# Splitting 42 matmuls of the last block into halves of 256 columns, which moves TensorE's instruction fetches by 84 instructions

## The chip, the cores and the metric

The kernel runs on one core of a Trainium2 chip. The metric is the device time of one execution in microseconds (us); a quoted time is a median of several executions. The profiled execution also has a span, from the first to the last instruction of the program; here the time is some 2 us longer than the span. All executions told of here are marked fast (single ones: unknown), and the granted clock of TensorE (PE in the profile), as the mean of an execution, is 0.998 to 1.0 everywhere; the lower values in some windows below stand behind its last matmul.

Executions of one kernel differ by several tenths of a microsecond, mostly because the first 40 us, where inputs are loaded, never run quite alike. So besides the times this document uses a distance that leaves the beginning out: **from the start of the last matmul to the end of the last store packet**, both taken from the single records of the trace. It is called the *tail* below.

## The reference

```python
x: (16, 512, 768)   w1: (768, 3072)   b1: (3072,)   w2: (3072, 768)
y = np.matmul(x, w1) + b1
y = 0.5 * y * (1.0 + erf(y / np.sqrt(2.0)))
return np.matmul(y, w2).astype(np.float32)
```

## The kernel before

The 8192 rows are worked through in eight blocks of 1024. Both products use a seven-product scheme (Strassen's, in Winograd's form) in place of eight block products. A block of the first product has twelve units (`Unit1`), each with seven products of three matmuls of 512 columns:

```python
class Unit1:
    F = RH          # 512
    C = KQ          # 3
    ...
    def mm(self, p, dst, first, c0, c1):
        A11, A12, A21, A22 = blocks(self.sb)
        a, slot = {1: (A11, B11), ...}[p]
        for c in range(c0, c1):
            nc.tensor.matmul(out=dst[:, 0:RH], lhsT=w1_op(self.wt, slot)[:, c, :],
                             rhs=a[:, c, :], start=first and c == 0,
                             stop=c == self.C - 1, skip_group_check=True)
```

The second product of the last six blocks has seven units (`Unit3`), each with seven products of twelve matmuls of 192 columns. The rest of the output is stored at the end: four stores of 384 KB while the very last unit runs, then that unit's `store_quarter`, its `store(0)` in `p3`, and two small ones in `last`, one on SyncE and one on ScalarE:

```python
def p3(u):
    u.mm(3, bZ, False, 0, u.C)
    ...
        nc.vector.tensor_tensor(out=u.c12(), in0=u.bank(bZ), in1=u.bank(w), op=ADD)
        if u.ends:
            u.store(0)                       # 384 KB, the fifth full store
...
def last(self, banks):
    for t in range(2):
        self.mm(4, banks[t], True, 0, self.C, (t,))
        o = self.dst[:, 1, t, 0, :]
        tt(o, banks[t][:, t * N4:(t + 1) * N4], o, ADD)
        (nc.sync, nc.scalar)[t].dma_start(out=orr[...], in_=o)      # 96 KB each
```

## Time and profile before

| | before |
|---|---|
| time, median of 3 runs | 852.42 us (852.32 to 852.53) |
| span of the profiled run | 850.5 us |
| TensorE busy | 842.8 us, 99% |
| TensorE's instruction fetches | 51 packets of 16 KiB |
| last matmul starts | 845.02 us |
| last fetch starts | 844.30 us |
| last store packet ends | 848.97 us |

The page, the groups, SyncE's last stores and the windows of the end are shown line by line in the prediction below. A window is a stretch of time, and its DMA share is the mean over the core's sixteen DMA engines, so that a share of 0.06 is one engine at work and fifteen idle. Two more lines of the time line of before are needed later, TensorE's last group and ScalarE's store (start, length, engine, line, operation, count):

```profile
844.12 1.15 PE L518 MATMUL bX<-arena 128*128 128x192 f16 x12
```

```profile
845.70 0.38 ACTq L529 DMA_DIRECT2D out_dram<-arena  x1
```

### The profile page before, as it was taken

Reading aid. Unit: us, or ns where it says so; the run is one execution under the profiler, and the core shown is the slowest. Engines: PE = TensorE matmul, PEld = TensorE weight load, DVE = VectorE, ACT = ScalarE, POOL = GpSimd, SP = SyncE. Lnnn points to the kernel's source line nnn. Section 1 sums busy time; section 2 is a strip of 40 time slices with the busy share of each in tenths; the row PEclk is TensorE's granted clock in tenths of the full one; section 3 lists DMA queues with packets and bytes.
Section 4 is the critical chain, followed back from the end, with each engine's and each line's share of the span. In section 5 each row is a group of like instructions: output and inputs, shape, how many; then the busy total and the mean of one; then the engine's idle time right before and its main releaser. Section 6 shows DMA issues by size and latency. Waiting matters only on the chain.

```text
span 850.5 us, 16682 instructions
## 1 busy us (share of the span) xinstructions
PE 842.8 (99%) x6504; PEld 573.4 (67%) x6504; DVE 673.3 (79%) x1134; ACT 426.3 (50%) x700; POOL 94.8 (11%) x151
## 2 busy tenths in 40 slices
PE   8999999999999999999999999999999999999997
PEld 5444445796544897449964599545995469944797
DVE  5766679777857997679967799668996699957997
ACT  4777763231287413773247721577126861277511
POOL 5021100042200002000020000210002100010000
PEclk9999999999999999999999999999999999999999
DMA  9998796699998699977999599995999949984497
GB/s 224 203 282 173 163 222 230 235 203 219 368 340 185 216 338 364 290 163 266 335 366 292 125 298 342 360 288 108 316 350 347 259 143 323 359 308 146 122 316 255
DMA packets 144819, 222.11 MB, mean 261 GB/s; under 512 B 61964, under 2 KB 85444, under 8 KB 144740
## 3 DMA queue, kind: packets, MB, share of 16 engines
q1 hardware_dynamic: 117392, 178.85, 66.6%
q0 software_dynamic: 27168, 42.08, 22.3%
q8 instruction: 51, 0.84, 0.4%
q14 instruction: 28, 0.23, 0.1%
q10 hardware_dynamic: 180, 0.11, 0.0%
HBM read 181.78 MB, written 49.45 MB: 272 GB/s over the span
## 4 chain that ended last, share of the span: by engine, by line
PE 98%; DMA 1%; ACT 0%; DVE 0%; SPq 0%; issue 0%
PE bY L414 21%; PE bY L518 15%; PE bX L414 14%; PE bX L518 10%; PE bW L414 7%; PE bZ L414 7%; PE bZ L518 5%; PE bW L518 5%; PE bY L457 4%; PE bZ L457 2%; PE bW L457 2%; PE bY L606 2%; PE bX L606 1%; PE bX L457 1%; DMA arena<-in_x_dram 1%; PE bZ L606 1%
## 5 line engine op out<-in xcount | busy, mean ns | idle before, releaser
L210 DVE TENSOR_TENSOR arena<-arena 128x1536 f16<-128x1536 f16 (+6 forms) x638 | 410.1, 674 | 5.7 <-ACT arena L335 0.9
L414 PEld LDWEIGHTS <-arena 128*128 128x128 f16 x1974 | 192.5, 98 | 224.0 <-issue 0.2
L518 PEld LDWEIGHTS <-arena 128*128 128x128 f16 x3528 | 292.1, 98 | 8.2
L414 PE MATMUL bY<-arena 128*128 128x512 f16 x846 | 214.4, 379 | 0.0
L637 DVE TENSOR_TENSOR arena<-bY,arena 128x512 f32<-128x512 f32 (+1 forms) x102 | 69.4, 681 | 118.1 <-PE bY L414 88.0
L630 ACT COPY bY<-bX 128x512 f32<-128x512 f32 (+1 forms) x145 | 79.6, 549 | 118.1 <-DVE arena L567 87.9
L518 PE MATMUL bY<-arena 128*128 128x192 f16 x1500 | 138.3, 246 | 0.0
L414 PE MATMUL bX<-arena 128*128 128x512 f16 x564 | 138.2, 379 | 0.0
L430 ACT ACTIVATE arena<-arena,b1t 128x1024 f16<-128x1024 f32 x94 | 108.0, 1149 | 51.6 <-DVE arena L665 51.6
L650 ACT COPY arena<-bW 128x512 f32<-128x512 f32 (+1 forms) x149 | 81.9, 550 | 92.9 <-PE bW L518 43.9
L518 PE MATMUL bX<-arena 128*128 128x192 f16 x1020 | 93.1, 246 | 0.0
L665 DVE TENSOR_TENSOR arena<-bZ,arena 128x512 f32<-128x512 f32 (+1 forms) x102 | 69.3, 679 | 21.4 <-PE bZ L414 18.2
L550 POOL DMA_DIRECT2D out_dram<-arena x42 | 30.5, 728 | 409.7 <-DVE arena L661 374.1
L414 PE MATMUL bW<-arena 128*128 128x512 f16 x282 | 76.2, 379 | 0.0
L414 PE MATMUL bZ<-arena 128*128 128x512 f16 x282 | 76.2, 379 | 0.0
L681 ACT COPY bZ<-bY 128x512 f32<-128x512 f32 (+1 forms) x60 | 31.8, 529 | 80.8 <-PE bY L457 30.0
L435 ACT ACTIVATE arena<-bX,b1t 128x512 f16<-128x512 f32 x94 | 64.0, 680 | 9.8 <-PE bX L414 9.7
L435 ACT ACTIVATE arena<-bY,b1t 128x512 f16<-128x512 f32 x94 | 63.3, 674 | 0.0
L457 PEld LDWEIGHTS <-arena 128*128 128x128 f16 x432 | 42.2, 98 | 28.0 <-issue 0.2
L319 POOL DMA_DIRECT2D arena<-in_x_dram x60 | 33.5, 626 | 156.3 <-DMA arena<-arena 146.9
L518 PE MATMUL bZ<-arena 128*128 128x192 f16 x504 | 48.5, 246 | 0.0
L518 PE MATMUL bW<-arena 128*128 128x192 f16 x504 | 48.5, 246 | 0.0
(63 smaller groups left out, 426.4 us busy)
## 6 DMA issues: line engine op xcount, KB each, us to landing
arena<-w2s SPq DMA_DIRECT2D x299, 288.0 KB, 4.6
arena<-w1s SPq DMA_DIRECT2D x72, 672.0 KB, 6.8
out_dram<-arena POOLq DMA_DIRECT2D x46, 384.0 KB, 7.1
w2s<-arena SPq DMA_DIRECT2D x49, 288.0 KB, 4.4
arena<-in_x_dram POOLq DMA_DIRECT2D x60, 192.0 KB, 7.7
w1s<-arena SPq DMA_DIRECT2D x12, 672.0 KB, 6.6
arena<-in_w_dram POOLq DMA_DIRECT2D x17, 384.0 KB, 8.4
out_dram<-arena SPq DMA_DIRECT2D x13, 384.0 KB, 2.5
```

Source lines behind the costliest of these rows:

```text
L210: nc.vector.tensor_tensor(out=o, in0=a, in1=b, op=op)
L319: nc.gpsimd.dma_start(out=xhs[t], in_=xr[:, sb * 8 + t, :])
L414: nc.tensor.matmul(out=dst[:, 0:RH], lhsT=w1_op(self.wt, slot)[:, c, :], rhs=a[:, c, :], start=first and c == 0, stop=c == self.C - 1, ski ...
L430: nc.scalar.activation(out=self.G[1][:, hi, :, :], in_=self.tmp, func=GELU, bias=b1t[:, 2 * hi + 1:2 * hi + 2])
L435: nc.scalar.activation(out=self.G[0][:, hi, row, :], in_=bank[:, 0:RH], func=GELU, bias=b1t[:, 2 * hi:2 * hi + 1])
L457: nc.tensor.matmul(out=dst[:, 0:N2], lhsT=a, rhs=w[:, :, c, :], start=first and c == 0, stop=c == self.C - 1, skip_group_check=True)
L518: nc.tensor.matmul(out=dst[:, t * N4:(t + 1) * N4], lhsT=a, rhs=w[:, c, :], start=first and c == 0 and t == ts[0], stop=c == NQ - 1, skip_ ...
L606: nc.tensor.matmul(out=dst[:, t * N4:(t + 1) * N4], lhsT=a, rhs=self.w[q][:, c, :], start=first and c == 0 and t == 0, stop=c == NQ - 1, s ...
L630: nc.scalar.copy(out=bY[u.g % 2][:, 0:u.F], in_=bX[u.g % 2][:, 0:u.F])
L637: nc.vector.tensor_tensor(out=u.c22(), in0=bY[u.g % 2][:, 0:u.F], in1=w[:, 0:u.F], op=ADD)
L650: nc.scalar.copy(out=w[:, 0:u.F], in_=bW[:, 0:u.F])
L665: nc.vector.tensor_tensor(out=u.c12(), in0=bZ[:, 0:u.F], in1=w[:, 0:u.F], op=ADD)
```

## The change

Units 1 and 2 of the last block's first product issue each matmul as two of 256 columns. The result is the same; 42 matmuls and their 42 weight loads are added, 84 instructions, so that every block of 256 instructions that TensorE fetches afterwards begins 84 instructions earlier in the work. The intent is to move the fetches, not to change the arithmetic.

```diff
                 a, slot = {1: (A11, B11), ...}[p]
+                w = RH // (2 if self.sb + 1 == nsb and self.k in (1, 2) else 1)
                 for c in range(c0, c1):
-                    nc.tensor.matmul(out=dst[:, 0:RH], lhsT=w1_op(self.wt, slot)[:, c, :],
-                                     rhs=a[:, c, :], start=first and c == 0,
-                                     stop=c == self.C - 1, skip_group_check=True)
+                    for r in range(0, RH, w):
+                        nc.tensor.matmul(out=dst[:, r:r + w], lhsT=w1_op(self.wt, slot)[:, c, :],
+                                         rhs=a[:, c, r:r + w], start=first and c == 0 and r == 0,
+                                         stop=c == self.C - 1, skip_group_check=True)
```

## The prediction

> **What bounds the kernel now.** I read the page first: busy time, queues and the chain of work that ended last.
>
> ```profile
> PE 842.8 (99%) x6504; PEld 573.4 (67%) x6504; DVE 673.3 (79%) x1134; ACT 426.3 (50%) x700; POOL 94.8 (11%) x151
> ...
> q8 instruction: 51, 0.84, 0.4%
> ...
> PE 98%; DMA 1%; ACT 0%; DVE 0%; SPq 0%; issue 0%
> ```
>
> TensorE is the bound: 842.8 of 850.5 us, 98% of the chain. The queue marked "instruction" moved 51 packets, 0.84 MB, so 16 KiB each; 6504 matmuls and 6504 weight loads in 51 pieces make 255 instructions a piece, so this queue is TensorE's own. That is the thing the change wants to shift. Does a fetch ever hold TensorE? The rows of groups say no: the columns after the bar are busy us, mean ns, then idle us before.
>
> ```profile
> L414 PE MATMUL bY<-arena 128*128 128x512 f16 x846 | 214.4, 379 | 0.0
> L518 PE MATMUL bY<-arena 128*128 128x192 f16 x1500 | 138.3, 246 | 0.0
> ```
>
> No idle time stands before either kind. I also took the distance from each matmul's start to the next one's: all the excess over the usual distance sums to 1.9 us in the whole run, 1.2 of it in the first 100 us; in the last block one step of 0.08 us stands out, at 815.25 us, and its like is found once in each of the five blocks before, exactly 103 us apart, while the fetches fall at another phase in every block. So no fetch costs TensorE anything, and what is left to gain lies outside its busy time: the first 2 us, and the 5.2 us between its last matmul (845.3) and the end (850.5).
>
> So I read the end closely: SyncE's time line of the last stores, then windows (columns: window, its length, busy us of PE, PEld, DVE, ACT, POOL, granted clock, DMA share, GB/s).
>
> ```profile
> 839.65 3.26 SPq L550 DMA_DIRECT2D out_dram<-arena  x4
> 843.91 0.37 SPq L556 DMA_DIRECT2D out_dram<-arena  x1
> 844.90 1.04 SPq L550 DMA_DIRECT2D out_dram<-arena  x1
> 846.04 0.42 SPq L529 DMA_DIRECT2D out_dram<-arena  x1
> ```
>
> ```profile
> 838.00:840.50 2.50, 2.50 (x34) 2.50 (x32) 2.50 (x5) 0.48 (x1) 0.00 (x0) 1.00 0.03 10
> 840.50:841.60 1.10, 1.10 (x16) 1.10 (x15) 1.00 (x3) 0.00 (x0) 0.00 (x0) 1.00 0.93 344
> 841.60:842.00 0.40, 0.40 (x8) 0.40 (x6) 0.40 (x2) 0.00 (x0) 0.00 (x0) 1.00 0.35 123
> 842.00:845.80 3.80, 3.27 (x40) 3.04 (x37) 3.18 (x8) 0.00 (x0) 0.00 (x0) 1.00 1.00 349
> 845.80:846.40 0.60, 0.00 (x0) 0.00 (x0) 0.00 (x0) 0.00 (x0) 0.00 (x0) 1.00 0.06 15
> 846.40:848.30 1.90, 0.00 (x0) 0.00 (x0) 0.00 (x0) 0.00 (x0) 0.00 (x0) 0.85 0.92 316
> 848.30:849.00 0.70, 0.00 (x0) 0.00 (x0) 0.00 (x0) 0.00 (x0) 0.00 (x0) 0.50 0.06 21
> ```
>
> The reader is to see the two windows with a DMA share of 0.06, one engine of sixteen: 845.8 to 846.4 and 848.3 to 849.0. One DMA engine is behind the other fifteen, and the program waits for it twice. The single packet records say why: at 844.297 us the last instruction fetch, 16,384 B, starts on one engine and takes 1.241 us; on that engine no data packet starts until 845.524, and the next four of 1,536 B start 0.16 us apart, where the usual distance is 0.062 us. And the store issued at 844.90 took 1.04 us to issue where the others took about 0.4; it ended (845.95) only after the slow engine had moved three more packets. The same shows earlier: of the ten other DMA issues on SyncE after 211 us that took over 0.75 us, nine began 0.2 to 1.2 us after a fetch had begun, and the tenth 0.04 us before one. The last packets of fifteen engines end by about 848.28, the last of the slow one at 848.97.
>
> **What the Trainium skill says.** "Runtime: NRT & Kernel Launch", section Instruction fetch mechanics: the queue is refilled in 16 KiB blocks of 256 instructions, by a DMA queue that the sequencer drives, at a cost that is mostly hidden. The trace agrees with the block and with hidden, for TensorE; not for the stores behind it. "DMA: Bandwidth & Descriptors", section Queues, rings and completion order: every DMA engine takes its queue rows in turn, packet by packet. The trace agrees: the 16 KiB packet is one turn of 1.24 us. "TensorE: Matmul & The Clock Gate", section Back-to-back issue gap: N/2.4 + 2.5 ns between isolated warm matmuls, which is 215.8 ns at 512 columns and 109.2 at 256. "Advanced Engine Details and Errata", section Engine Queue Depths: 64 for TensorE; no view shows the depth directly.
>
> **The change, part by part.** *Added work.* Units 1 and 2 of the last block have 7 products of 3 matmuls each: 42 matmuls of 512 columns become 84 of 256, with 42 more weight loads. The order of the built program agrees: 13,093 TensorE rows for 13,009, and nothing moved on another engine. Both sizes stand in the trace of before (columns: start, length, what):
>
> ```profile
> 18.54 0.82 PE L786 MATMUL bY<-arena 128*128 128x256 f16 x6
> 19.19 0.82 PE L786 MATMUL bW<-arena 128*128 128x256 f16 x6
> ...
> 22.46 0.81 PE L414 MATMUL bW<-arena 128*128 128x512 f16 x3
> 23.11 0.81 PE L414 MATMUL bY<-arena 128*128 128x512 f16 x3
> ```
>
> Start to start that is 0.65 us for 6 matmuls of 256 and for 3 of 512; the records give 109 and 216 ns as medians, in agreement with the skill. So each split costs 2 x 109 - 216 = 2 ns, 42 of them 0.084 us, all on TensorE's path. The weight load (98 ns) hides under 109 ns, as it does under the 82.6 ns of the 192-column matmuls. **Cost: +0.09 us.**
>
> *Moved fetches.* Every fetch boundary after unit 2 comes 84 instructions earlier. In the last stretch a pair of weight load and matmul takes 0.0826 us, so 42 pairs are 3.47 us: the last fetch goes from 844.30 to about 840.8 on the old clock. It may be earlier still: the sequencer runs ahead of the array, and before the change it was held by the matmul at 842.14, which waits for VectorE's read of the bank (ended 842.05); the new boundary lies before that matmul. Up to 1.5 us earlier, then: 839.3 to 841. I take 840.4. No fetch is added: about 100 instructions, fewer than 256, remain behind it.
>
> *What the place is worth.* The slow engine is busy without a break from 842.0 to 848.97. Its data in that time: 64 packets of 1,536 B at 0.062 us and 32 of 768 B at 0.033, 3.97 + 1.06 = 5.03 us; the fetch with its slowed neighbours is the rest, 6.97 - 5.03 = 1.94 us. A fetch inside that stretch would cost the same wherever it falls. What counts is how much of it falls into time in which this engine would idle: from 838.0 to 840.5 (share 0.03) and the lull from 841.6 to 842.0. Starting at 840.4, with 1.24 us of its own and 0.43 us for four slowed packets behind it, then 80 packets of 1,536 B (4.96) and 32 of 768 B (1.06) and 0.07 for small packets, the engine is done at 840.4 + 1.24 + 0.43 + 4.96 + 1.06 + 0.07 = 848.16 instead of 848.97: **0.8 us saved**. Starting at 840.9 it is 0.3 to 0.4. If the fetch is wholly over before 840.5, the other fifteen engines are the bound: with the store issued in 0.4 us at 844.90 and 590 KB left (384 + two of 96 KB) at some 365 GB/s from about 845.9, they end near 847.6, so 1.35 saved at most.
>
> Sum, weighed towards the middle: -0.7 + 0.09 = -0.6 us: **851.8 us**.
>
> **The rivals.** *A, only the added work counts:* the fetch lands between 842 and 845, or the lag is made elsewhere too. For it: the stretch from 842.0 is full, and the skill calls fetches hidden. Against it: 3.47 us reach before 842 by simple counting. Time 852.5. *B, the fetch escapes altogether into the idle 2.5 us.* For it: the sequencer's lead; the change looks cut to fit this gap. Against it: the straight shift puts it some 0.3 us too late. Time 851.1 to 851.2. *C, TensorE pays:* weight loads exposed, 42 x 98 ns = 4.1 us, or a fetch that now comes late. Against it: 256-column matmuls at 109 ns with a load each, and no fetch of 51 that held TensorE, with spacings from 9 to 32 us. Time 856. *D, moved fetches delay ring loads* before the end. They are issued ten products (10 us) ahead and land in 4.6 us at the median; a lag of 1.9 us doesn't reach TensorE.
>
> **Range and chances.** The ends are A (852.5) and B with a little more (851.0); most weight goes to a fetch that begins between 839.5 and 841. Runs of before spread over 0.2 us. 2% would be 17 us, and nothing here moves even 2 with any likelihood, save C at small odds: faster 0.01, same 0.98, slower 0.01.
>
> **What would show it.** In the changed profile: 51 instruction packets again; TensorE's last matmul some 0.09 us later; the last fetch between 839.4 and 841.1; the fifth full store issued in less than 1.04 us; the window of share 0.06 after 845.8 shorter or gone; the gap between the last matmul and the end down from 5.2 to about 4.5 us. Wrong would be: the last fetch after 842 (then A), or a lone late engine at the end although the fetch was early (then the lag has another cause), or TensorE's end later by more than 0.3 us (then C).

## The result, and the profile after

| | before | after |
|---|---|---|
| time, median of 6 runs | 852.37 us (852.18 to 852.68) | 851.49 us (851.18 to 851.71) |
| span of the profiled run | 850.5 us | 849.0 us |
| last matmul starts | 845.02 us | 844.93 us |
| last fetch starts, lasts | 844.30, 1.24 us | 839.49, 0.93 us |
| tail: last matmul's start to last packet's end | 3.94 us | 2.60 us |

The median fell by 0.88 us. The ratio is 0.9989, with a 95% interval of 0.9976 to 1.0002. Ratios in this document compare runs of the same rounds and are not quite the ratio of the medians quoted. The six runs of each do not overlap, yet the interval includes 1; what makes the gain certain is the traces.

The page after, the lines that answer to those of before: TensorE's busy time, its fetch queue, and the chain that ended last.

```profile
PE 843.8 (99%) x6546; PEld 577.9 (68%) x6546; DVE 673.6 (79%) x1134; ACT 426.3 (50%) x700; POOL 95.2 (11%) x151
...
q8 instruction: 51, 0.84, 0.4%
...
PE 95%; DMA 4%; DVE 0%; POOL 0%; issue 0%; DVEq 0%
```

TensorE is as full as before, with 42 matmuls more and the same 51 fetches. (The 4% of DMA in the chain are inputs at the start.) The end is where the kernels differ. SyncE's last stores after:

```profile
839.55 3.26 SPq L552 DMA_DIRECT2D out_dram<-arena  x4
843.82 0.37 SPq L558 DMA_DIRECT2D out_dram<-arena  x1
844.81 0.37 SPq L552 DMA_DIRECT2D out_dram<-arena  x1
845.27 0.45 SPq L531 DMA_DIRECT2D out_dram<-arena  x1
```

The fifth full store is issued in 0.37 us instead of 1.04, and the small one behind it starts at 845.27 instead of 846.04. The windows of the end, with the columns as in the prediction:

```profile
838.80:839.40 0.60, 0.60 (x10) 0.60 (x8) 0.60 (x1) 0.00 (x0) 0.00 (x0) 1.00 0.00 0
839.45:840.40 0.95, 0.95 (x15) 0.95 (x13) 0.95 (x3) 0.00 (x0) 0.00 (x0) 1.00 0.06 17
...
845.70:846.30 0.60, 0.00 (x0) 0.00 (x0) 0.00 (x0) 0.00 (x0) 0.00 (x0) 1.00 0.98 348
846.30:847.50 1.20, 0.00 (x0) 0.00 (x0) 0.00 (x0) 0.00 (x0) 0.00 (x0) 1.00 0.96 321
847.50:848.90 1.40, 0.00 (x0) 0.00 (x0) 0.00 (x0) 0.00 (x0) 0.00 (x0) 1.00 0.00 0
```

The two lines that answer to TensorE's last group and ScalarE's store of before:

```profile
844.02 1.15 PE L520 MATMUL bX<-arena 128*128 128x192 f16 x12
```

```profile
845.60 0.39 ACTq L531 DMA_DIRECT2D out_dram<-arena  x1
```

Both stand 0.10 us earlier than before (844.12 and 845.70), so the work that feeds the stores accounts for 0.1 us of the 1.5 that the span lost; the rest is in the stores.

In the windows, the single engine's work at 839.45 is the fetch; its packet is the only one in that window. It is over before the first store packet starts. Where before had 0.06 after 845.8, there is now 0.98, and where before had one engine still working until 848.97, nothing moves after 847.53.

### The profile page after: what moved, and what is told of

It is laid out like the page before. It is cut to its first block, busy times and chain, and to the rows that moved or that the text cites. A ratio compares the mean times of both kernels' runs of the same rounds, so it can differ in the third digit from the quotient of the medians. Undisturbed runs are those within 1.5% of the kernel's fastest.

```text
span 849.0 us, 16767 instructions
## 1 busy us (share of the span) xinstructions
PE 843.8 (99%) x6546; PEld 577.9 (68%) x6546; DVE 673.6 (79%) x1134; ACT 426.3 (50%) x700; POOL 95.2 (11%) x151
## 4 chain that ended last, share of the span: by engine, by line
PE 95%; DMA 4%; DVE 0%; POOL 0%; issue 0%; DVEq 0%
PE bY L416 21%; PE bY L520 15%; PE bX L416 14%; PE bX L520 10%; PE bZ L416 7%; PE bW L416 7%; PE bZ L520 5%; PE bW L520 5%; PE bY L459 4%; DMA arena<-in_x_dram 3%; PE bZ L459 2%; PE bW L459 2%; PE bY L608 2%; DMA arena<-in_w_dram 1%; PE bX L608 1%; PE bX L459 1%
## 5 line engine op out<-in xcount | busy, mean ns | idle before, releaser
L416 PE MATMUL bY<-arena 128*128 128x512 f16 (+1 forms) x864 | 214.5, 375 | 0.1
L416 PE MATMUL bX<-arena 128*128 128x512 f16 (+1 forms) x576 | 138.3, 375 | 0.0
L416 PE MATMUL bZ<-arena 128*128 128x512 f16 (+1 forms) x288 | 76.2, 375 | 0.0
L416 PE MATMUL bW<-arena 128*128 128x512 f16 (+1 forms) x288 | 76.2, 375 | 0.0
```

What stands on the lines that cost most here:

```text
L416: nc.tensor.matmul(out=dst[:, r:r + w], lhsT=w1_op(self.wt, slot)[:, c, :], rhs=a[:, c, r:r + w], start=first and c == 0 and r == 0, stop= ...
```

## The experiments

All the kernels gave the right result. "Fetch" and "tail" are relative to the start of the last matmul; the fetch is the last one that begins before the end. The medians are of 4 runs (6 for the changed kernel, one for nop30 and nop36), those of before of 7 runs in the same rounds (6 beside the changed kernel).

| kernel | instructions added | fetch | tail | time | before beside it | ratio |
|---|---|---|---|---|---|---|
| before | 0 | -0.73 us | 3.94 us | | | |
| changed | 84, by splits | -5.44 | 2.60 | 851.49 us | 852.37 us | 0.9989 |
| nop84 | 84, empty | -5.47 | 2.60 | 851.08 | 852.28 | 0.9986 |
| split_early | 84, by splits, earlier block | -5.39 | 2.60 | 851.71 | 852.28 | 0.9992 |
| nop40 | 40, empty | -3.10 | 3.18 | 851.77 | 852.28 | 0.9995 |
| act_store | 0 | -0.36 | 3.99 | 852.49 | 852.28 | 1.0005 |
| nop20 | 20, empty | -0.55 | 3.90 | 852.83 | 852.58 | 1.0000 |
| nop212 | 212, empty | -9.28 | 2.60 | 851.05 | 852.58 | 0.9979 |
| nop256 | 256, empty | -0.35 | 3.99 | 852.19 | 852.58 | 0.9992 |
| after_again | 84, by splits | -5.59 | 2.59 | 851.24 | 852.58 | 0.9981 |
| nop30 | 30, empty | -0.46 | 3.85 | 852.50 | | |
| nop36 | 36, empty | -3.39 | 3.07 | 851.61 | | |

The times of before scatter too (852.23 to 854.40 in the second group), and only the intervals of nop212 and after_again leave out 1, so the tail, from one profile of each kernel (two of the changed one), carries the argument. The theory under test is the prediction's: the last fetch makes one DMA engine late, and the time is saved because the fetch now falls where that engine is idle. The rivals: the split matmuls or added instructions help by themselves; or what costs is the held issue of the fifth store.

### nop84: the shift without the splits

The kernel before, with two instructions that do nothing behind each of 42 matmuls, from unit 1 on. (Those units are interleaved, so the last few stand behind matmuls of unit 3 and not of unit 2, as the expectation has it; it makes no difference to the count.)

```diff
+        pads = [84]
         class Unit1:
...
                                      stop=c == self.C - 1, skip_group_check=True)
+                    for _ in range(2 if self.sb + 1 == nsb and self.k and pads[0] else 0):
+                        nc.tensor.nop(hint="pad", nofuse=True)
+                        pads[0] -= 1
```

> The kernel before with 84 TensorE instructions that do nothing, two behind each of the 42 matmuls of the same two units, and no matmul split. If the place of the last instruction fetch makes the gain, the fetch must start near 839.5 us as in the changed kernel, the last store packet end near 847.5 instead of 849.0, and the time be 851.4 us (0.9 to 1.1 below the kernel before), some 0.09 less than with splits. If the split matmuls themselves help (other bank or queue timing), nothing is gained: 852.4. If the do-nothing instructions cost array time, above 852.5.

Measured: 851.08 us, ratio 0.9986, tail 2.60 us, the same as with splits to a hundredth. The profile counts 84 instructions more than before, so they reached the chip; the stretch of matmuls that is split in the changed kernel took 12.967 us, where before it took 12.965, so they cost the array nothing. The first of them is recorded 2.05 us before the matmul in front of it starts: that is how far the sequencer, the part of TensorE that reads its instructions, was ahead of the array there. Two windows of this kernel, the fetch's and the end's:

```profile
839.50:840.45 0.95, 0.95 (x14) 0.95 (x12) 0.95 (x3) 0.00 (x0) 0.00 (x0) 1.00 0.06 17
847.60:849.00 1.40, 0.00 (x0) 0.00 (x0) 0.00 (x0) 0.00 (x0) 0.00 (x0) 0.76 0.00 0
```

No matmul was split and the whole gain is there: the splits are only a way to count to 84. The rival of the splits falls.

### split_early: the same splits, three blocks earlier

```diff
-                w = RH // (2 if self.sb + 1 == nsb and self.k in (1, 2) else 1)
+                w = RH // (2 if self.sb + 4 == nsb and self.k in (1, 2) else 1)
```

> The same 42 splits, but in the block three before the last, so that the last block's matmuls are those of the kernel before and only the fetch boundaries stand where the change puts them. Fetch place theory: last fetch near 839.5, time 851.5, as the changed kernel. Rival (what helps is a different timing inside the last block's first product): 852.5.

Measured: 851.71 us, tail 2.60 us, fetch 5.39 us before the last matmul. The interval of the ratio, 0.9978 to 1.0007, includes 1; the tail is what agrees. In these two places it does not matter where the 84 instructions stand. Here the fetch took 1.19 us and ended 0.27 us after the first store packet had started, and still cost nothing: what little lateness it left was gone before the end.

### act_store: the late engine stays late, the held issue is taken away

```diff
-            def store(self, r):
+            def store(self, r, eng=None):
...
-                eng = nc.sync if self.sb + 1 == nsb and self.p != 2 else nc.gpsimd
+                eng = eng or (nc.sync if self.sb + 1 == nsb and self.p != 2 else nc.gpsimd)
...
                 if u.ends:
-                    u.store(0)
+                    u.store(0, nc.scalar)
```

> The kernel before, fetches unmoved, but the last large store (384 KB at 844.90 us) is issued on ScalarE's queue[...], instead of SyncE's. If what costs time is that the issue is held for 1.04 us[...], the end comes 0.6 us earlier: 851.7. If the late engine's own work (no idle time from 842.0 to 848.97) sets the end, the issue gets short and the lull after 845.8 goes, but the last packet still ends near 848.9: 852.3 (+-0.2).

Measured: 852.49 us, ratio 1.0005, tail 3.99 us. The fifth full store's issue on ScalarE, then two windows of the end:

```profile
845.93 0.43 ACTq L550 DMA_DIRECT2D out_dram<-arena  x1
```

```profile
846.90:848.60 1.70, 0.00 (x0) 0.00 (x0) 0.00 (x0) 0.00 (x0) 0.00 (x0) 1.00 0.99 341
848.75:850.00 1.25, 0.00 (x0) 0.00 (x0) 0.00 (x0) 0.00 (x0) 0.00 (x0) 1.00 0.07 25
```

The issue took 0.43 us instead of 1.04, and fifteen engines went on with little pause. They then waited 1.3 us for the sixteenth, where before they had waited 0.65 us in the middle and 0.7 at the end. So the held issue is a symptom. The end is set by the late engine's own queue of work. That the rival is wrong is shown twice more: nop256 and nop30 below, too, have an issue of 0.37 us, and tails of 3.99 and 3.85.

### nop212: no fetch among the stores at all

As nop84 with `pads = [212]`: with blocks of 256 this is 44 instructions later than before.

> 212 do-nothing instructions: with blocks of 256 this puts the boundaries 44 instructions later than in the kernel before, so that the last one falls behind the kernel's last matmul and no fetch is left among the last stores. Theory: 51 fetches or 50, the last more than 9 us before the last matmul; last packet 2.60 us after the last matmul's start as in the changed kernel; time 851.0 to 851.3, and less scattered than the changed kernel, whose fetch lies next to the stores. Rival (more instructions than 84 gain no more, or cost): 852.4 or above.

Measured: 851.05 us, ratio 0.9979 with an interval of 0.9964 to 0.9994, tail 2.60 us, the last fetch 9.28 us before the last matmul. One window of its end:

```profile
847.55:849.00 1.45, 0.00 (x0) 0.00 (x0) 0.00 (x0) 0.00 (x0) 0.00 (x0) 1.00 0.00 0
```

Taking the fetch out of the stretch gains no more than moving it into the idle time before the first store packet, so in the changed kernel the fetch costs nothing any more. The expected smaller scatter did not show: 850.80 to 851.30, twice as wide as that of the changed kernel beside it (851.12 to 851.37).

### nop256: once round, back to the start

As nop84 with `pads = [256]`.

> 256 do-nothing instructions, a whole block: one fetch more (52), and the boundaries in the tail where the kernel before has them. Theory: the gain is gone. Last fetch 0.3 to 0.9 us before the last matmul's start, last packet 3.9 to 4.0 after it, time 852.3 (ratio 1.000 +-0.0003). Rival (added instructions as such make the gain): 851.1 as with 84.

Measured: tail 3.99 us, last fetch 0.35 us before the last matmul, 52 fetches. The queue's line of the page, and a window of the end:

```profile
q8 instruction: 52, 0.85, 0.4%
```

```profile
847.65:848.90 1.25, 0.00 (x0) 0.00 (x0) 0.00 (x0) 0.00 (x0) 0.00 (x0) 1.00 0.07 25
```

Three times as many added instructions as the change, and the late engine is back. What counts is where the added instructions put the boundary within a block of 256, not how many they are. (Its time, 852.19, lies 0.4 us below the median of before in these rounds, with an interval of the ratio from 0.9977 to 1.0007. That difference is not explained; the tail, 3.99 against 3.94, is no shorter than before.)

### nop40, nop20, nop30, nop36: a step, not a slope

As nop84 with `pads = [40]`, `[20]`, `[30]` and `[36]`.

> 40 do-nothing instructions in place of 84. The boundary then lies behind the matmul that waits for VectorE until 842.05 us, so the last fetch should start between 842.8 and 844, inside the stretch in which the slow DMA engine is never idle. Theory: no gain, 852.4 (+-0.2), one engine still late at the end, last packet near 848.9. Rival (any earlier fetch helps in proportion, 40/84 of the gain): 852.0. Rival (the added instructions help by themselves): 851.9 or less.

> 20 do-nothing instructions. Runs so far: no shift, fetch 0.4 to 0.7 us before the last matmul starts; 40, 3.1 us before; 84, 5.4 us before. If TensorE's sequencer is held by the matmul that waits for VectorE until about 3.0 us before the last matmul, and the fetch starts some 2.2 us after that whatever the count behind the wait, 20 instructions change nothing: fetch at -0.4 to -0.9, last packet 3.9 to 4.0 us after the last matmul's start, time as the kernel before (ratio 1.000). If the fetch moves with the count (20 instructions are 0.83 us of matmuls), it starts at -1.3 to -1.6; being inside the stretch without idle time, the end should still be near 3.9 (the prediction's claim), or, if a fetch costs less the earlier it falls, 3.5 to 3.8.

> 30 do-nothing instructions, one look. At 20 the last fetch began 0.55 us before the last matmul's start, at 40 it began 3.10 before. If the sequencer is held at one waiting matmul, the change between the two is a step, not a slope: at 30 the fetch begins either at -0.4 to -0.9 or at -2.9 to -3.6, nothing between, and the last packet comes at 3.9 to 4.0 or at 3.1 to 3.3. My reckoning of the boundary (34 instructions needed to bring it before the waiting matmul) says -0.4 to -0.9. A slope would give about -1.8.

> 36 do-nothing instructions, one look. By the same reckoning the boundary is now just before the waiting matmul: fetch at -2.9 to -3.3, last packet at 3.1 to 3.3 after the last matmul's start. A slope between 20 and 40 would give about -2.6; a step that lies later than reckoned, -0.4 to -0.9.

nop40 was a miss: the fetch came at 841.86 us, 1 to 2 us earlier than expected, and the tail fell to 3.18 us instead of staying near 3.9. Its last window with one engine at work is shorter, 847.50 to 848.10:

```profile
847.50:848.10 0.60, 0.00 (x0) 0.00 (x0) 0.00 (x0) 0.00 (x0) 0.00 (x0) 1.00 0.08 24
```

The other three followed from what nop40 had taught. With 0, 20 and 30 instructions the fetch begins 0.73, 0.55 and 0.46 us before the last matmul, so not earlier with more instructions (act_store and nop256, whose boundary stands where before has it, have 0.36 and 0.35); with 36 and 40 it begins 3.39 and 3.10 before. Six instructions (0.25 us of matmuls) move the fetch by 2.9 us. A fetch that followed the count could not do that; a sequencer that is held at one instruction can. The step falls where I had reckoned the matmul that waits for VectorE, whose release comes 2.97 us before the last matmul in all of these traces. Two numbers of that reckoning were fitted to the runs before it: where the boundary lies, and some 2.2 us from crossing it to the packet. That it is this wait which holds the sequencer is therefore well supported, but no run removed the wait itself.

### after_again

> The changed kernel, unedited, once more, beside the others: time 851.2 to 851.7, last packet 2.60 us after the last matmul's start when the fetch is over before the stores begin; if the fetch starts later than 5.2 us before the last matmul in this execution, up to 3.1.

Measured: 851.24 us, ratio 0.9981, tail 2.59 us. The first set of the changed kernel had runs near 851.2 and near 851.7; these four lie from 851.12 to 851.37. In each of its two profiles (executions of 851.18 and 851.37 us) the fetch was over before the stores began; no execution near 851.7 was profiled, so what makes the upper level is open.

## Why the prediction was right or wrong

It said 851.8 us (851.0 to 852.5), and 851.49 was measured: right in direction and cause, about two thirds of the gain in size (0.6 of 0.9 us).

- **No fetch holds TensorE: right.** The last block's step of 0.08 us is there again in the changed kernel at 815.16 us, while the fetches have moved; its cause was not looked for.
- **The splits' cost of 0.09 us: right.** In the changed trace the 84 halves start 109.2 ns apart, and the stretch of work that holds them took 13.056 us where before it took 12.965, 0.09 longer. The last matmul still starts 0.09 us earlier than before, not later, because this execution's beginning happened to be quicker. That expected sign of the prediction was below the scatter of the first 40 us.
- **One late engine sets the end, not the held issue: right**, and shown by act_store, nop256 and nop30. (The prediction's count of ten other slow issues on SyncE leaves out, without saying so, the 40 transposes issued there after 211 us, which take 1.2 us or more wherever the fetches fall.)
- **The place of the fetch: the step that was mis-sized.** "I take 840.4" was 839.49 in the trace. The range named beside it, 839.3 to 841, held it, but the middle was 0.9 us too late. The step from 30 to 36 instructions is the likely reason why straight counting (3.47 us) fell short: before the change the sequencer was held, and it is not held at the new boundary; the prediction had named this, up to 1.5 us, and allowed for 0.4 of it. The fetch moved by 4.7 us (from -0.73 to -5.44).
- **What the place is worth: 0.8 us predicted, 1.34 measured** in the tail (3.94 to 2.60). It follows from the step above. The case that happened is rival B, "the fetch escapes altogether"; its ceiling of 1.35 us, worked out from 590 KB at 365 GB/s, was met. Its time of 851.1 to 851.2 was that of the profiled run (851.18), while the median stayed 0.3 us above it.
- **"A fetch inside that stretch would cost the same wherever it falls": wrong at its edge, untested in its middle.** Against a tail of 2.60, fetches that begin 0.35 to 0.73 us before the last matmul cost 1.25 to 1.39 us, but those of nop36 and nop40, at 3.39 and 3.10 before, cost 0.47 and 0.58. These two begin in the lull just before the stretch (841.61 and 841.86 us) and run on into it. The packet records show most of the difference, because the slow data packets ahead of a fetch cost time too. In nop256 one packet of 0.168 us and seven of about 0.116 stand ahead of the fetch, where 0.065 is usual; by their starts they lose 0.5 us, the fetch takes 0.92, and four slow packets behind it lose 0.4, together 1.8. In nop40 the slow packets ahead of the fetch (0.12 to 0.19 us) fall before the end of the lull, which takes them up; what is left is 0.88 for the fetch and 0.4 behind it, together 1.3. That is 0.5 to 0.6 of the 0.8 us between the two costs. The rest, and why packets beside a fetch are slow, is left open. (Which packets share the fetch's engine is inferred from their starts; the records do not name the engine.)
- **Rival C (TensorE pays): absent.** The weight loads of the halves stay hidden.

The Trainium skill's statement ("Runtime: NRT & Kernel Launch", Instruction fetch mechanics) that a fetch's cost is mostly hidden holds for TensorE: in none of the twelve traces is any step from matmul to matmul after 250 us more than 0.11 us over the usual one, with some 40 fetches in each. It fails for the stores that share a DMA engine with a fetch near the end: up to 1.39 us of the tail.

## What to carry to other kernels

When a kernel ends in a burst of stores, look at the instruction queue's packets in the last few microseconds: one 16 KiB packet on one of sixteen engines can make that engine the last to finish, and a window with a DMA share of one sixteenth shows it. Some empty instructions well before the end moved such a fetch at no cost to a full TensorE (nop84 and nop212 took 851.1 us; the changed kernel took 851.24 beside nop212, a difference within their scatter). How far it moves has to be measured: here it came in a step. The effect hangs on the instruction count, so a later edit of TensorE's program can undo or restore it by chance.

## What the Trainium skill lacked or had wrong

- "Runtime: NRT & Kernel Launch", Instruction fetch mechanics: it tells the cost of a block boundary for the fetching engine alone. Here the packet of 16 KiB took 0.88 to 2.00 us (0.93 us alone in the changed kernel's idle window), and a fetch among the last stores lengthened the tail by up to 1.39 us.
- The same section says that the next page is fetched while the current one is executed, but not how far ahead, nor that the lead changes in steps. Here 0 to 30 added instructions left the last fetch 0.36 to 0.73 us before the last matmul, and 36 put it at 3.39.
- "DMA: Bandwidth & Descriptors", Queues, rings and completion order: the turn by turn sharing of an engine agrees with the traces, but not told is that data packets beside a fetch slow down: 0.16 to 0.18 us for four behind a late one, 0.12 for four to seven ahead of it, where 0.065 is usual. Nor does it tell that a store's issue can take longer when one of sixteen engines is behind: 1.04 and 1.00 us instead of 0.37 in before and nop20, though 0.37 in nop256 and nop30, whose fetches began later.
- "TensorE: Matmul & The Clock Gate", Back-to-back issue gap: the formula for the isolated gap, 109.2 ns at 256 columns and 215.8 at 512, fits this full stream of weight loads and matmuls (109.2 and 216 ns), for which the page gives 131 ns at 512.
